# Other SBUF offsets for the operands of the matmuls: bytes left free in five pools

## The chip, the core and the metric

The kernel runs on one core of a Trainium2 chip. A core has a matrix engine (TensorE, PE in the profile; its weight loads are listed apart as PEld), a vector engine (VectorE, DVE), a scalar engine (ScalarE, ACT), a general engine (GpSimd, POOL) and a queue that issues most transfers (SyncE, SP). They share a memory of 128 partitions, SBUF; TensorE writes its results to a second memory, PSUM. The metric is the time of one execution on the device in microseconds (us), lower is better.

A matmul has two operands in SBUF. The *stationary* one (128 x 128 here) is loaded into the array by a weight load, the *moving* one (512, 384, 256 or 128 columns here) is then streamed past it. An address in this document is the byte offset of an operand within a partition, and an *offset* is that address modulo 256.

## The reference

One layer of a diffusion backbone, in float32, for 256 context tokens and 2048 latent tokens of width 1024:

```
h = rms_norm(x, norm1_g) * (1 + scale1) + shift1
q, k, v, f = split(h @ w_in)                      # 512 columns each
q, k = rms_norm(q), rms_norm(k)                   # rotary on the latent tokens
s = einsum('bqhmd,bkhmd->bhmqk', q, k) * scale    # 4 heads x 2 halves, 512 cached keys + 2048
p = softmax(s);  a = p[:, :, 0] - lam * p[:, :, 1]
attn = rms_norm(a @ v);  four = real(fft2(f)) @ w_four
x = x + gate1 * (concat(attn, four) @ w_out)
h = rms_norm(x, norm2_g) * (1 + scale2) + shift2
x = x + gate2 * (square(relu(h @ w1)) @ w2)       # 4096 hidden columns
```

The context tokens attend to themselves only. The modulation vectors come from `silu(c) @ w_mod + b_mod`. Outputs are the two groups of tokens and the new keys and values of the context.

## The kernel before

Each float32 product is made of three passes in the type fp32r: an operand is split into a high part and the rest, and `mm3` (lines 87 to 90) adds high x high (L88), high x low (L89) and low x high (L90) in PSUM. The stages follow each other and PE works through them in one order:

- **Projection** (33 to 476 us of the span): for each of 18 tiles of 128 tokens, four groups of 512 columns (`proj`). The activations `hh`, `hl` are stationary, the weights `wh`, `wl` are moving; products go to `pj`. 1728 matmuls of 512 columns on L88 to L90.
- **Fourier** part, to about 530 us; float32 matmuls without the split.
- **Attention** (530 to 1256 us): `fill` (L1065) multiplies a query tile `Q` (stationary) by 512 columns of keys `KS` (moving), 1272 matmuls into `Ss`. DVE takes the maxima (L1070), ACT the exponentials (L1089), POOL combines the two softmax halves (L1104, L1105), PE transposes the result (L1120, against the constant `ident`), ACT and DVE split it into `ah`, `al` (L1127, L1132), and PE multiplies by the values: `V` stationary, `ah` and `al` moving with 256 columns, 1536 matmuls on L88 to L90 into `po`. Keys, values and queries of a head are loaded by SP.
- **Output projection** (1256 to 1480 us): `mh`, `ml` stationary, the weights `woh`, `wol` moving with 512 columns, 864 matmuls, also into `po`. The weights' two halves of 512 output columns lie in different pools.
- **First MLP matrix** (1480 to 2184 us): seven products p = 1 to 7 of a Strassen scheme over blocks; the weights `oph..W`, `opl..W` are stationary, the tokens `mhh`, `mhl` are moving with 384 columns (L1728 to L1730), 4032 matmuls. p = 1 and 2 go to `pA`, 6 and 7 to `pB`, 5 and 3 to `pC`, 4 to `pD`. The tokens of p = 1 and 6 lie in the pool `hpa`, the others in the pools `hp[p]`.
- **Second MLP matrix** (2184 us to the end): the squared activations `sh`, `sl` are stationary and go round three buffers (`s_prep`: two in the pool `ms2s`, one in `t6`); the weights are moving with 512 columns and go round buffers in `ms2` (`oph..T`, `opl..T`) and in `y_w` (`th..T`, `tl..T`). 3024 matmuls on L88 to L90 into `ps`.

SBUF is handed out by pools. Pools of one side of the memory stand behind each other in the order in which they are opened, and the tiles of a pool in the order of their first use, so a byte more in one pool moves every tile behind it. Tiles start at multiples of 32 bytes. `reuse_waits="tile"` makes a new tile wait only for the users of the old tiles that it overlaps.

The lines that hand out the operands, among others:

```
qg, kg = cst("qg", [P, P]), cst("kg", [P, P])
t = ak.tile([P, self.nk], F32R, tag=f"KS{m}_{self.s}", name=f"KS{m}{self.nm}")
self.Q = at.tile([P, 2, 2, 256], F32R, tag="Q", name=f"Q{self.nm}", bufs=3)
mh = tm.tile([P, KD, P], F32R, tag="mh", name=f"mh{i}")
pool, bufs = (ms2s, 2) if m % 3 < 2 else (own["t6"], 1)
```

Of the kernel before, what the change touches and what calls it, by code (L numbers as in the profile page):

```python
# [11 lines left out]
F32 = mybir.dt.float32  # L12
# [7 lines left out]
P = 128  # L20
# [21 lines left out]
def body(tc, a, out):  # L42
    nc = tc.nc
    ctx = ExitStack()
    with ctx:
        const = ctx.enter_context(tc.tile_pool(name="const", bufs=1))
        dram = ctx.enter_context(tc.tile_pool(name="dram", bufs=1, space=DRAM))

        def cst(name, shape, dt=F32):
            return const.tile(shape, dt, tag=name, name=name)  # L50
# [27 lines left out]
        scale1 = cst("scale1", [P, KD, 2])  # L78
        scale2 = cst("scale2", [P, KD, 2])
        cols = cst("cols", [P, P])  # L80
        qg, kg = cst("qg", [P, P]), cst("kg", [P, P])
        nlam = cst("nlam", [P, 1])

        def pow_mhalf(dst, src, n):
            nc.gpsimd.tensor_tensor(dst, src, mhalf[:, :n], op=ALU.pow)
# [17 lines left out]
        def setup_cond(pool, pps, rows):  # L103
# [7 lines left out]
            nc.vector.tensor_copy(cols, pr)  # L111
            nc.vector.tensor_scalar_mul(cols[:, 96:97], cols[:, 96:97], 1.0 - LAM_INIT)

        def load_gains(pool):
            for t, n in ((qg, "q_norm_g"), (kg, "k_norm_g")):
                nc.gpsimd.dma_start(t[:, 0:64], a[n].partition_broadcast(P).rearrange("p o d -> p (o d)"))
            lq = pool.tile([P, 512], F32, tag="ff", name="lq", bufs=4)[:, 0:256].rearrange("p (n d) -> p n d", d=64)
            for i, n in enumerate(("lambda_q1", "lambda_q2", "lambda_k1", "lambda_k2")):
                nc.gpsimd.dma_start(lq[:, i, :], a[n].partition_broadcast(P).rearrange("p o d -> p (o d)"))
            return lq  # L120

        def setup_gains(pool, lq):
            for t, s in ((qg, 0.125), (kg, 1.0)):
                if s != 1.0:
                    nc.vector.tensor_scalar_mul(t[:, 0:64], t[:, 0:64], s)
                nc.vector.tensor_copy(
                    t[:, 64:128].rearrange("p (x h j) -> p x h j", h=2, j=16),
                    t[:, 0:64].rearrange("p (x h j) -> p x h j", h=2, j=16)[:, :, ::-1, :])
            nc.vector.tensor_mul(lq[:, 0:2, :], lq[:, 0:2, :], lq[:, 2:4, :])
            ls = pool.tile([P, 2], F32, tag="ls", name="ls")  # L130
            nc.vector.tensor_reduce(ls, lq[:, 0:2, :], axis=AX.X, op=ALU.add)
            nc.scalar.activation(ls, ls, AF.Exp)
            nc.vector.tensor_sub(nlam, ls[:, 1:2], ls[:, 0:1])
            nc.vector.tensor_scalar_add(nlam, nlam, -LAM_INIT)
# [111 lines left out]
        with ExitStack() as c1:  # L246
# [62 lines left out]
            def qk_post(i, ms=(0, 1), dst=None):  # L309
                s = i < 2  # L310
                if i not in RP:
                    rope_load(i)
                rp = RP.get(i)
                res = QK.setdefault(i, [])
                for m in ms:
                    gt = (qg, kg)[m]
                    if (i, m) not in QN:
                        qk_norm(i, m)
                    qn = QN.pop((i, m))
                    o = dst[m] if dst else po.tile([P, 512], F32, tag="qo", name=f"qo{i}_{m}", bufs=2)  # L320
                    if s:
                        nc.vector.tensor_mul(o.rearrange("p (g d) -> p g d", d=64),
                                             qn.rearrange("p (g d) -> p g d", d=64),
                                             gt[:, 0:64].unsqueeze(1).to_broadcast([P, 8, 64]))
                        if m == 1:
                            nc.sync.dma_start(out[2][i * P:i * P + P], o)
                    else:
                        tb = p1.tile([P, P], F32, tag="tb", name=f"tb{i}_{m}")
                        nc.vector.tensor_mul(tb, rp, gt)
                        nc.vector.tensor_mul(o.rearrange("p (g d) -> p g d", d=64),  # L330
                                             qn.rearrange("p (g d) -> p g d", d=64),
                                             tb[:, 0:64].unsqueeze(1).to_broadcast([P, 8, 64]))
                        t = t2(f"qt{i}_{m}")
                        tv = t.rearrange("p (g x h j) -> p x g h j", x=2, h=2, j=16)
                        qv = qn.rearrange("p (g x h j) -> p x g h j", x=2, h=2, j=16)
                        bv = tb[:, 64:128].rearrange("p (x h j) -> p x h j", h=2, j=16)
                        for x in range(2):
                            nc.vector.tensor_mul(tv[:, x], qv[:, x, :, ::-1, :],
                                                 bv[:, x].unsqueeze(1).to_broadcast([P, 8, 2, 16]))
                        nc.vector.tensor_add(o, o, t)  # L340
                    res.append(o)
# [111 lines left out]
            with tc.manual_schedule():  # L453
# [36 lines left out]
                with tc.tile_pool(name="p0h", bufs=6, reuse_waits="tile") as halves:  # L490
# [61 lines left out]
                    for k in range(KD):  # L552
# [20 lines left out]
                        if k in (1, 3):  # L573
                            b = k // 2
# [403 lines left out]
        with ExitStack() as c3_:  # L978
# [18 lines left out]
            class Head:  # L997
# [16 lines left out]
                def load_v(self):  # L1014
                    s, h, ak = self.s, self.h, self.ak
                    self.V = ak.tile([P, self.nkt, 2, P], F32R, tag=f"V_{s}", name=f"V{self.nm}")
                    nc.sync.dma_start(f32(self.V), vd[s][h])
                    self.vf = {}
                    if not s:
                        for kb in FULL:  # L1020
                            t = ak.tile([P, 2, P], F32, tag=f"vf{kb}", name=f"vf{kb}{self.nm}")
                            r = (kb - 4) * P
                            nc.sync.dma_start(t, vs[r:r + 2 * P, self.hc].rearrange("(t p) e -> p t e", p=P))
                            self.vf[kb] = t

            class Group:
                def __init__(self, hd, g):
# [423 lines left out]
        def h_parts(b, p):  # L1451

            src = HR.pop((b, p))
            pool = hpa if p in (1, 6) else hp[p]
            hi = pool.tile([P, 4, 384], F32R, tag=f"mhh{p}", name=f"mhh{b}_{p}")
            lo = pool.tile([P, 4, 384], F32R, tag=f"mhl{p}", name=f"mhl{b}_{p}")
            HO[b, p] = hi, lo
            src = src if isinstance(src, list) else [(slice(0, 4), src)]

            def high():  # L1460
# [45 lines left out]
        with c3o, ExitStack() as c4, ExitStack() as c4x, ExitStack() as c4w:  # L1506
# [2 lines left out]
            tm = c4.enter_context(tc.tile_pool(name="o_m", bufs=2, reuse_waits="tile"))  # L1509
            wl1 = c4.enter_context(tc.tile_pool(name="o_wl", bufs=1, reuse_waits="tile"))  # L1510
            t4 = c4.enter_context(tc.tile_pool(name="o_t", bufs=2, reuse_waits="tile"))
            wh1 = c4.enter_context(tc.tile_pool(name="o_wh", bufs=1, reuse_waits="tile"))
            tg = c4.enter_context(tc.tile_pool(name="o_g", bufs=2, reuse_waits="tile"))
            tx = c4x.enter_context(tc.tile_pool(name="o_x", bufs=2, reuse_waits="tile"))
# [172 lines left out]

        with c5r, ExitStack() as c5:
            hp.update((p, c5.enter_context(tc.tile_pool(name=f"m_h{p}", bufs=1, reuse_waits="tile"))) for p in (3, 4, 5, 7, 2))
            t5 = c5.enter_context(tc.tile_pool(name="m_t", bufs=2, reuse_waits="tile"))  # L1690
            pp = c5.enter_context(tc.tile_pool(name="m_p", bufs=2, space=PSUM, reuse_waits="tile"))
            PSB, U, G = {}, {}, {}
# [420 lines left out]
```

## Time and profile before

| | |
|---|---|
| median of 3 runs | 2883.29 us (2882.81 to 2885.51) |
| profiled execution | 2884.46 us |
| its span on the core | 2882.3 us |
| PE busy, with 15109 matmuls | 2849.2 us, 99% |
| weight loads (PEld) | 2465.0 us, 86% |
| DVE busy | 2017.5 us, 70% |
| ACT busy | 1547.8 us, 54% |
| POOL busy | 1063.5 us, 37% |
| granted TensorE clock | 0.999 of full speed |

A matmul's row in the trace lasts from its start to a modelled end, and the next one starts before that end. What a matmul costs PE in a dense stretch is therefore not the length of its row but the distance from its start to the start of the next one; below it is called the *interval*. PE counts as busy in the gap of up to some 160 ns that the modelled ends leave open. For the same reason a group's mean length (the second to last number of a row of groups) stands some 160 ns above the interval.

### The profile page before, as it was taken

The numbers are of one execution on the slowest core, as the hardware profiler recorded it, in microseconds if no ns is written. First come the engines' busy times: TensorE is split into PE (matmuls) and PEld (weight loads), VectorE is DVE, ScalarE is ACT, GpSimd is POOL, SyncE is SP. The second block draws the span as 40 slices with busy tenths as digits, with TensorE's granted clock in tenths as the row PEclk, the third lists the DMA queues.
The fourth block names the chain that finished last, engine by engine and source line by source line (L and its number), as shares of the span: only waits on it lengthen the run. The fifth ranks groups of instructions, "written<-read, shape, count | busy, mean of one in ns | idle before, by whom it ended". The sixth has DMA issues, their size and how long they took to land.

```text
span 2882.3 us, 43198 instructions
## 1 busy us (share of the span) xinstructions
PE 2849.2 (99%) x15109; PEld 2465.0 (86%) x15109; DVE 2017.5 (70%) x3376; ACT 1547.8 (54%) x3505; POOL 1063.5 (37%) x873
## 2 busy tenths in 40 slices
PE   8999999999999999999999999999999999999999
PEld 5888787688888888888889999999998888888887
DVE  7767776898988989864477777778775353445554
ACT  4333323798998989853356565556554332232221
POOL 1112113699998999942223333333331000000000
PEclk9999999999999999999999999999999999999999
DMA  7877887531211312036777677667747464345653
GB/s 283 216 194 190 228 210 229 191 112 38 72 69 46 113 38 98 21 116 204 241 215 236 218 247 229 219 220 240 227 166 254 146 201 139 132 143 186 206 199 110
DMA packets 392779, 492.93 MB, mean 171 GB/s; under 512 B 26467, under 2 KB 306384, under 8 KB 389490
## 3 DMA queue, kind: packets, MB, share of 16 engines
q1 hardware_dynamic: 387136, 479.73, 52.7%
q0 software_dynamic: 1872, 7.28, 0.8%
q10 hardware_dynamic: 3554, 3.17, 0.4%
q8 instruction: 119, 1.95, 0.3%
q14 instruction: 98, 0.80, 0.1%
HBM read 312.58 MB, written 179.59 MB: 171 GB/s over the span
## 4 chain that ended last, share of the span: by engine, by line
PE 91%; DVE 3%; DMA 2%; ACT 2%; issue 1%; POOL 0%; SPq 0%; ACTq 0%; DVEq 0%; POOLq 0%
PE Ss L1065 10%; PE ps L88 8%; PE ps L89 8%; PE ps L90 8%; PE pts L1120 5%; PE pj L88 4%; PE pj L89 4%; PE pj L90 4%; PE po L90 4%; PE po L88 4%; PE po L89 4%; PE pA L1728 2%; PE pA L1729 2%; PE pB L1729 2%; PE pB L1728 2%; PE pB L1730 2%
## 5 line engine op out<-in xcount | busy, mean ns | idle before, releaser
L1070 DVE TENSOR_REDUCE mxs<-Ss 128x1 f32<-128x512 f32 x636 | 413.2, 685 | 62.5 <-PE Ss L1065 50.6
L1405 DVE TENSOR_TENSOR sl<-sr,sh 128x768 fp32r<-128x768 f32 x168 | 161.7, 964 | 337.8 <-ACT sh L1404 336.3
L1105 POOL TENSOR_TENSOR P0s<-P0s,P1s 128x1024 f32<-128x1024 f32 (+2 forms) x128 | 378.7, 2958 | 10.7
L1404 ACT CAST sh<-sr 128x768 fp32r<-128x768 f32 x168 | 140.2, 836 | 424.8 <-PE ps L89 424.8
L1770 POOL TENSOR_TENSOR gs<-g,g 128x384 f32<-128x384 f32 x48 | 69.6, 1450 | 469.5 <-ACT g L1740 420.3
L88 PE MATMUL pj<-wh,hh 128*128 128x512 f32 x576 | 231.4, 402 | 4.5 <-DVE qn L305 2.4
L1089 ACT ACTIVATE P1s<-Ss,mxs 128x512 f32<-128x512 f32 x318 | 215.2, 694 | 36.1 <-DVE mxs L1073 36.1
L89 PE MATMUL ps<-tlT,sh 128*128 128x512 f32 x585 | 229.3, 392 | 0.0
L89 PE MATMUL pj<-wl,hh 128*128 128x512 f32 x576 | 229.2, 398 | 0.0
L88 PE MATMUL ps<-thT,sh 128*128 128x512 f32 x585 | 229.0, 391 | 0.0
L90 PE MATMUL pj<-wh,hl 128*128 128x512 f32 x576 | 228.8, 398 | 0.0
L90 PE MATMUL ps<-thT,sl 128*128 128x512 f32 x585 | 227.7, 389 | 0.0
L1089 ACT ACTIVATE P0s<-Ss,mxs 128x512 f32<-128x512 f32 x318 | 214.1, 690 | 5.5 <-DVE mxs L1073 4.8
L1065 PE MATMUL Ss<-KS1s,Qs 128*128 128x512 f32 x636 | 196.2, 420 | 5.8 <-ACT P0s L1089 3.1
L1065 PE MATMUL Ss<-KS0s,Qs 128*128 128x512 f32 x636 | 195.4, 420 | 2.4 <-ACT P1s L1089 2.4
L1120 PEld LDWEIGHTS pts<-ident,P0s 128*128 128x128 f32 x1280 | 157.7, 140 | 42.7 <-issue 2.1
L1120 PE MATMUL pts<-ident,P0s 128*128 128x128 f32 x1280 | 190.5, 272 | 0.7 <-ACT P1s L1089 0.7
L1739 ACT ACTIVATE g<-uz 128x384 f32<-128x384 f32 x144 | 75.8, 527 | 200.9 <-DVE uz L1762 174.4
L1104 POOL TENSOR_SCALAR P1s<-P1s,tots 128x1024 f32<-128x1024 f32 (+2 forms) x128 | 171.8, 1342 | 5.8
L1132 DVE TENSOR_TENSOR als<-pts,ahs 128x512 fp32r<-128x512 f32 x256 | 165.9, 681 | 6.9 <-ACT ahs L1127 6.6
L88 PE MATMUL ps<-ophT,sh 128*128 128x512 f32 x423 | 165.7, 392 | 1.1 <-DVE uz L1762 1.1
L90 PE MATMUL ps<-ophT,sl 128*128 128x512 f32 x423 | 165.7, 392 | 0.0
(536 smaller groups left out, 8057.5 us busy)
## 6 DMA issues: line engine op xcount, KB each, us to landing
sr<-sd SPq DMA_DIRECT2D x84, 768.0 KB
a<-in_w SPq DMA_DIRECT2D x184, 256.0 KB
sd<-gs SPq DMA_DIRECT2D x192, 192.0 KB
sd<-g SPq DMA_DIRECT2D x144, 192.0 KB
wm<-in_w_mod SPq DMA_DIRECT2D x32, 512.0 KB
Qs<-qd SPq DMA_DIRECT2D x32, 512.0 KB
b<-in_w SPq DMA_DIRECT2D x64, 256.0 KB
b<-tsum SPq DMA_DIRECT2D x64, 256.0 KB
```

Of the source, the lines that this page charges most:

```text
L88: nc.tensor.matmul(ps, lh, rh, start=first, stop=False)
L89: nc.tensor.matmul(ps, lh, rl, start=False, stop=False)
L90: nc.tensor.matmul(ps, ll, rh, start=False, stop=last)
L1065: nc.tensor.matmul(S[:, :w], self.Q[:, x, m, j * P:j * P + P], self.hd.KS[m][:, b * 512:b * 512 + w], start=(x == 0), stop=(x == 1))
L1070: nc.vector.tensor_reduce(self.mx[j][:, m, b:b + 1], self.S[j, m, b], axis=AX.X, op=ALU.max)
L1089: nc.scalar.activation(dst, S, AF.Exp, bias=self.mx[j][:, m, 6:7], accum_out=self.sm[j][:, m, b:b + 1])
L1104: nc.gpsimd.tensor_scalar(p, p, tot[:, 3:4], 0.0, op0=ALU.mult, op1=ALU.add)
L1105: nc.gpsimd.tensor_add(d, d, p)
L1120: nc.tensor.transpose(pt[:, c:c + P], self.p0[j][:, (kb + t) * P:(kb + t + 1) * P], ident)
L1132: nc.vector.tensor_sub(t, self.pt[kb], f32(self.A[kb][0]))
L1404: nc.scalar.copy(hi, src)
L1405: nc.vector.tensor_sub(lo, src, f32(hi))
```

## The change

The change adds a helper `shift` that takes a tile nobody uses out of a pool, calls it in seven places, and takes the two gain tiles `qg`, `kg` out of the pool of constants and into `p1`. No instruction is added, removed or moved: the instructions of PE, DVE, ACT, POOL and SP stand in the same order in both programs, and the waits of PE and DVE are the same too. Because a few tiles now overlap other old tiles, one semaphore wait less stands before two ACT exponentials and one POOL addition of the first attention groups and before a load of context keys on SP, and one wait for POOL more before one ACT cast (`mhh` of p = 7, first block, L1462).

```
@@ -78,8 +78,13 @@
-        qg, kg = cst("qg", [P, P]), cst("kg", [P, P])
         nlam = cst("nlam", [P, 1])
+
+        def shift(pool, nbytes, nm):
+
+            pool.tile([P, nbytes // 4], F32, tag=f"shift{nm}", name=f"shift{nm}", bufs=1)
+
+        shift(const, 192, "c")
@@ -111,7 +116,12 @@
+        GN = []
+
         def load_gains(pool):
+            shift(pool, 64, "p")
+            GN.extend(pool.tile([P, P], F32, tag=f"{x}g", name=f"{x}g", bufs=1) for x in "qk")
+            qg, kg = GN
@@ -120,7 +130,7 @@
-            for t, s in ((qg, 0.125), (kg, 1.0)):
+            for t, s in zip(GN, (0.125, 1.0)):
@@ -313,7 +323,7 @@
-                    gt = (qg, kg)[m]
+                    gt = GN[m]
@@ -1022,6 +1032,8 @@
                             self.vf[kb] = t
+                        if h == 0:
+                            shift(ak, 192, "k")
@@ -1452,9 +1464,13 @@
             pool = hpa if p in (1, 6) else hp[p]
+            if pool is hpa and not b and p == 6:
+                shift(hpa, 64, "a")
             hi = pool.tile([P, 4, 384], F32R, tag=f"mhh{p}", name=f"mhh{b}_{p}")
             lo = pool.tile([P, 4, 384], F32R, tag=f"mhl{p}", name=f"mhl{b}_{p}")
             HO[b, p] = hi, lo
+            if pool is hpa and not b and p == 6:
+                shift(hpa, 64, "b")
@@ -1509,6 +1525,7 @@
             t4 = c4.enter_context(tc.tile_pool(name="o_t", bufs=2, reuse_waits="tile"))
+            shift(t4, 128, "o")
@@ -1687,6 +1704,7 @@
             hp.update((p, c5.enter_context(tc.tile_pool(name=f"m_h{p}", bufs=1, reuse_waits="tile"))) for p in (3, 4, 5, 7, 2))
+            shift(hp[3], 64, "h")
```

What comes of it are other offsets. This table is worked out from the addresses that the pools gave in the two built programs; "distance" is the stationary operand's offset less the moving one's, modulo 256.

| matmuls, columns | moving | stationary | before: moving / stationary, distance | after |
|---|---|---|---|---|
| projection, 1728 x 512 | wh, wl | hh, hl | 224 / 32, 64 | 224 / 224, 0 |
| scores, 1272 x 512 | KS | Q | 160 / 32, 128 | 224 / 224, 0 |
| attention by values, 1536 x 256 | ah, al | V | 96 / 160, 64 | 32 / 224, 192 |
| transposes of P0, 1280 x 128 | ident | P0 | 128 / 32, 160 | 128 / 224, 96 |
| output projection, columns 512 to 1023, 288 x 512 | woh | mh, ml | 160 / 32, 128 | 224 / 224, 0 |
| the same, 144 x 512 | wol | mh | 32 / 32, 0 | 224 / 224, 0 |
| output projection, columns 0 to 511, 432 x 512 | woh, wol | mh, ml | 160 / 32, 128 | 224 / 224, 0 |
| first MLP matrix, p = 1 (`pA`), 576 x 384 | mhh, mhl | ophW, oplW | 224 / 224, 0 | 96 / 224, 128 |
| first MLP matrix, p = 6 (`pB`), 576 x 384 | mhh, mhl | ophW, oplW | 224 / 224, 0 | 160 / 224, 64 |
| first MLP matrix, the rest, 2880 x 384 | mhh, mhl | ophW, oplW | 32 / 224, 192 | 32 / 224, 192 |
| second MLP matrix, 846 x 512 | ophT, oplT | sh, sl in `ms2s` | 224 / 224, 0 | 224 / 224, 0 |
| second MLP matrix, 423 x 512 | ophT, oplT | sh, sl in `t6` | 224 / 32, 64 | 224 / 224, 0 |
| second MLP matrix, 1170 x 512 | thT, tlT | sh, sl in `ms2s` | 32 / 224, 192 | 224 / 224, 0 |
| second MLP matrix, 585 x 512 | thT, tlT | sh, sl in `t6` | 32 / 32, 0 | 224 / 224, 0 |

Every tile that moves does so by a multiple of 64 bytes; addresses in PSUM do not change.

## The prediction

> **What bounds the kernel now.** I read the page's busy shares and its chain first, then the stages.
>
> ```profile
> PE 2849.2 (99%) x15109; PEld 2465.0 (86%) x15109; DVE 2017.5 (70%) x3376; ACT 1547.8 (54%) x3505; POOL 1063.5 (37%) x873
> ...
> PE 91%; DVE 3%; DMA 2%; ACT 2%; issue 1%; POOL 0%; SPq 0%; ACTq 0%; DVEq 0%; POOLq 0%
> ```
>
> PE is busy for 99% of the span and is 91% of the chain that ended last. A change without a single new instruction can gain only where PE's own instructions follow each other faster. The stages, from the windows view (projection; attention; output projection; first and second MLP matrix):
>
> ```profile
> core 0: us, PE busy (x) PEld busy (x) DVE busy (x) ACT busy (x) POOL busy (x), PEclk, DMA share, GB/s
> 33.00:480.00 447.00, 444.22 (x2053) 360.03 (x2054) 322.93 (x586) 154.19 (x329) 86.39 (x68) 0.99 0.78 208
> 565.00:1256.00 691.00, 685.40 (x4470) 590.95 (x4469) 611.90 (x1196) 618.28 (x1729) 627.37 (x506) 1.00 0.19 65
> 1256.00:1480.00 224.00, 222.34 (x1071) 183.24 (x1070) 121.12 (x163) 90.68 (x211) 59.60 (x54) 1.00 0.70 215
> 1480.00:2184.00 704.00, 702.42 (x4044) 700.81 (x4043) 537.51 (x823) 419.55 (x786) 239.22 (x189) 1.00 0.68 223
> 2184.00:2882.00 698.00, 692.82 (x3026) 567.65 (x3024) 329.89 (x434) 204.04 (x290) 5.75 (x4) 1.00 0.51 168
> ```
>
> Four of the five leave the other engines at 76% or less and the transfers at 0.78, so time that PE saves there is saved. In attention DVE, ACT and POOL are at 89 to 91%: a gain there may partly turn into waiting. The clock stands at 0.99 to 1.00 everywhere, so it explains no difference between stages.
>
> **Does the offset matter?** The second MLP matrix answers it, since its three buffers of `sh` alternate between two offsets within a few microseconds, with the same instructions. From the timeline, the first matmul of each stretch:
>
> ```profile
> 2296.82 0.39 PE L88 MATMUL ps<-ophT,sh 128*128 128x512 f32 x1
> 2304.99 0.40 PE L88 MATMUL ps<-ophT,sh 128*128 128x512 f32 x1
> 2309.19 0.39 PE L88 MATMUL ps<-ophT,sh 128*128 128x512 f32 x1
> 2315.34 0.40 PE L88 MATMUL ps<-thT,sh 128*128 128x512 f32 x1
> 2317.42 0.39 PE L88 MATMUL ps<-thT,sh 128*128 128x512 f32 x1
> 2321.51 0.39 PE L88 MATMUL ps<-thT,sh 128*128 128x512 f32 x1
> 2329.75 0.39 PE L88 MATMUL ps<-ophT,sh 128*128 128x512 f32 x1
> ```
>
> One buffer serves 18 matmuls (two k, three row tiles, three passes). By the table of offsets, the first stretch is 36 matmuls at distance 0: 8.17 us / 36 = 226.9 ns each. Then 18 at distance 64: 4.20 / 18 = 233.3. Then 27 at distance 0: 6.15 / 27 = 227.8. After nine more at 192 come 18 at distance 0 with other weights: 4.09 / 18 = 227.2, and 36 at 192: 8.24 / 36 = 228.9. So distance 0 costs 227.4, distance 64 costs 5.9 ns more, distance 192 costs 1.5 more. Distance 128 shows in the output projection, where one half of the weights has `wol` at distance 0 and the other half has not:
>
> ```profile
> 1290.15 0.39 PE L89 MATMUL po<-wol,mh 128*128 128x512 f32 x1
> 1294.96 0.39 PE L89 MATMUL po<-wol,mh 128*128 128x512 f32 x1
> 1295.18 0.39 PE L90 MATMUL po<-woh,ml 128*128 128x512 f32 x1
> 1300.06 0.40 PE L90 MATMUL po<-woh,ml 128*128 128x512 f32 x1
> ```
>
> Seven triples with one matmul at distance 0: 4.81 / 21 = 229.0 ns on average. Seven triples at distance 128 throughout: 4.88 / 21 = 232.4. The neighbours of a matmul share in its gain, so I use averages over triples alone. These differences repeat each time a buffer comes round, under the same clock and instructions: I take the distance as their cause.
>
> **The change, part by part.** Intervals after the change are taken as 227.4 for all 512-column matmuls.
>
> *Projection.* All 1728 stand at distance 64. A dense run of 54 of them, up to the next transpose:
>
> ```profile
> 150.18 0.39 PE L90 MATMUL pj<-wh,hl 128*128 128x512 f32 x1
> 162.78 0.38 PE L347 MATMUL ptckT<-ident,ck 128*128 128x128 f32 x2
> ```
>
> 12.60 / 54 = 233.3, exactly the price of distance 64 above, though DVE and the transfers are far busier here. 1728 x 5.9 = **10.2 us**. DVE (72%) and ACT (34%) keep up.
>
> *Second MLP matrix.* 423 x 5.9 = 2.5 and 1170 x 1.5 = 1.8, together **4.3 us**. 1431 matmuls stay at distance 0.
>
> *Output projection.* 432 x (229.0 - 227.4) + 432 x (232.4 - 227.4) = 0.7 + 2.2 = **2.9 us**.
>
> *Scores.* 1272 at distance 128. In the view by source line, minimum / median / maximum length:
>
> ```profile
> L89 PE MATMUL ps<-oplT,sh x423: 387/389/398, 2184.4 to 2877.3; 128*128 128x512 f32 x141
> L89 PE MATMUL pj<-wl,hh x576: 388/394/628, 33.8 to 475.8; 128*128 128x512 f32 x192
> L1065 PE MATMUL Ss<-KS0s,Qs x636: 387/397/505, 530.1 to 1222.6; 128*128 128x512 f32 x159
> ```
>
> A row's length follows its interval: the median is 389 where most are at distance 0, 394 at distance 64, 397 in the scores. So they do pay; I take the 5.0 ns of distance 128: 1272 x 5.0 = 6.4 us of PE work. How much is kept is open, since PE waits here:
>
> ```profile
> 853.53 0.63 PE L1065 MATMUL Ss<-KS0s,Qs 128*128 128x512 f32 x2
> 853.99 0.27 PE L1120 MATMUL pts<-ident,P0s 128*128 128x128 f32 x1
> ...
> 854.78 0.28 PE L88 MATMUL po<-ahs,Vs 128*128 128x256 f32 x1
> 855.69 0.28 PE L90 MATMUL po<-ahs,Vs 128*128 128x256 f32 x1
> 856.07 0.73 PE L1065 MATMUL Ss<-KS1s,Qs 128*128 128x512 f32 x2
> ```
>
> Two scores take 0.46 us, eight value matmuls 0.91 (114 ns each), but the ninth is followed only after 0.38 us: some 0.26 us in which PE waits for ACT and DVE to free a score buffer, hidden under the modelled ends and counted as busy. Such waits shrink with nothing that PE saves if they come from ACT and DVE. With those at 90% I keep two thirds: **4.2 us** (bounds 0 and 6.4).
>
> *Values.* 1536 matmuls of 256 columns go from distance 64 to 192. No row shows 192 at this size. By the 512-column rows it would gain 4.4 ns; but the 114 above is already near what streaming 256 columns takes (227.4 / 2 = 113.7), which leaves little. Bounds: a gain of 2 ns (from a mean near 116) or a loss of as much as 6, the size of the step at 512 columns; within a stage that waits. I take **0**, bounds -3 and +9 us.
>
> *First MLP matrix.* 1152 matmuls of 384 columns leave distance 0, half for 128, half for 64. First matmuls of twelve:
>
> ```profile
> 1484.89 0.33 PE L1728 MATMUL pA<-mhh,ophW 128*128 128x384 f32 x1
> 1486.96 0.34 PE L1728 MATMUL pB<-mhh,ophW 128*128 128x384 f32 x1
> ...
> 1495.24 0.34 PE L1728 MATMUL pA<-mhh,ophW 128*128 128x384 f32 x1
> 1497.35 0.33 PE L1728 MATMUL pB<-mhh,ophW 128*128 128x384 f32 x1
> 1499.43 0.33 PE L1728 MATMUL pC<-mhh,ophW 128*128 128x384 f32 x1
> ```
>
> Distance 192 costs 2.07 / 12 = 172.5; distance 0 costs 2.11 / 12 = 175.8 in `pA` but 2.08 / 12 = 173.3 in `pB`. So here distance 0 is no advantage, and more than the offset plays a part. Best case: `pA` falls to 173, 576 x 2.5 = 1.4 us gained. Worst case: both pay what 64 and 128 cost at 512 columns over a floor of 173, 576 x (5.9 + 5.0 - 2.5) = 4.8 us lost. The stage has no cover, PE is all of it. I take a loss of **2.0 us**, a little over the middle of the two, the nearest rows at those distances being the 512-column ones.
>
> *Transposes.* They change their distance too, but their length is the same where the operand stands at 32 (`P0s`) and at 224 (`qo`), so nothing is put in:
>
> ```profile
> L1120 PE MATMUL pts<-ident,P0s 128*128 128x128 f32 x1280 | 190.5, 272 | 0.7 <-ACT P1s L1089 0.7
> L347 PE MATMUL ptqT<-ident,qo 128*128 128x128 f32 x64 | 9.6, 272 | 0.0
> ```
>
> *Waits.* The dropped ones concern transfers long landed; the new wait of one ACT cast is for POOL work of the stage before. Nothing.
>
> *Sum.* -10.2 - 4.3 - 2.9 - 4.2 + 0 + 2.0 = -19.6 us. The profiled execution took 2884.5 (span 2882.3 and 2.2 around it), 1.2 above the median of 2883.3; 2884.5 - 19.6 - 1.2 = 2863.7, so **2864 us**. Extremes of this case: all gains kept and the best bounds, -10.2 - 4.3 - 2.9 - 6.4 - 3 - 1.4 = -28.2 (2855); scores worth nothing, the values two thirds of their loss and the first MLP its worst, -17.4 + 6 + 4.8 = -6.6 (2877).
>
> [...]
>
> **The rivals.**
>
> *Only alternation shows a cause.* Projection and scores never alternate; their 233 and 232 could come from the denser traffic of DVE, ACT and transfers. Then only -4.3 - 2.9 + 2.0 = -5.2 remains: 2878. Against it: 233.3 is met to the tenth in a stage with half the DVE load. 0.09.
>
> *No effect.* The third buffer could be slow for where it lies, not for its offset (an area of memory beyond the 256 bytes, as the two figures of `pA` and `pB` at equal distance suggest). Then the new addresses draw anew: about 2883. Against it: `sh`, `wol` and the projection lie in quite different places and agree. 0.05. [...]
>
> *Slower: another engine in attention.* Every tile of that stage moves, those of POOL too:
>
> ```profile
> L1105 POOL TENSOR_TENSOR P0s<-P0s,P1s 128x1024 f32<-128x1024 f32 (+2 forms) x128 | 378.7, 2958 | 10.7
> ```
>
> POOL is busy for 627 of 691 us. Were its instructions to lengthen by 10% they would fill the stage, and from about 14% on they outweigh the gain: at 15%, 721 - 691 = 30 us more, less 15.4 kept elsewhere: 2898. Against it: both of its tiles move by the same 832 bytes. 0.04.
>
> **Chances.** The likeliest case 0.82 (about 0.02 of it less than 0.2% faster). 0.2% (5.8 us) is about what a measurement of this kernel can tell from no change. Faster 0.80 + 0.04 of the first rival = 0.84; same 0.02 + 0.05 + 0.04 = 0.11; slower 0.05, with 0.01 of the second. The range takes the likeliest case's bounds, cut at 2876 above: 2855 to 2876.
>
> **What would show it.** The lengths of `pj` and `Ss` rows fall to a median of 389; the stretches of `ps` lose their steps; the projection ends some 10 us earlier; `pA`/`pB` rows of 336 move up if 384 columns pay. I am wrong if `pj` keeps 394, if attention's 691 us don't shrink, or if the first MLP stage grows beyond 709.

## The result, and the profile after

The changed kernel takes 2871.26 us (median of 6 runs, 2869.99 to 2873.0) against 2883.53 us before (6 runs, 2882.81 to 2885.51). The ratio is 0.9957, with a 95% interval of 0.9944 to 0.9970: 12.3 us less. 2864 us were predicted, with a range of 2855 to 2876.

The profiled execution of the changed kernel took 2872.75 us, with a span of 2870.6. The changed file is longer at the top: `mm3` is now on lines 93 to 95, the scores are on L1077, the first MLP matrix on L1746 to L1748. The busy shares and the chain of the page of after:

```profile
PE 2836.0 (99%) x15109; PEld 2471.3 (86%) x15109; DVE 2015.4 (70%) x3376; ACT 1548.1 (54%) x3505; POOL 1063.7 (37%) x873
...
PE 54%; DVE 1%; DMA 0%; issue 0%; ACT 0%; SPq 0%; POOL 0%; DVEq 0%; POOLq 0%
```

PE lost 13.2 us of busy time, DVE 2.1, ACT and POOL did not change by more than 0.3, and the weight loads gained 6.3; the number of instructions is the same. The shares of the chain add up to 55% here, so it was followed only about half way back; what it holds is PE.

Where the time went is read best from the first matmul of each stage (projection, end of the projection, output projection, first and second MLP matrix). The timeline of before:

```profile
33.20 0.80 PE L88 MATMUL pj<-wh,hh 128*128 128x512 f32 x1 [1.98 <-DVE hh L544]
476.24 1.02 PE L777 MATMUL pabE<-c,E 128*128 128x256 f32 x4
1256.21 0.39 PE L88 MATMUL po<-woh,mh 128*128 128x512 f32 x1
1480.70 0.34 PE L1728 MATMUL pA<-mhh,ophW 128*128 128x384 f32 x1
2184.14 0.39 PE L88 MATMUL ps<-ophT,sh 128*128 128x512 f32 x1
```

and the timeline of after:

```profile
33.15 0.79 PE L93 MATMUL pj<-wh,hh 128*128 128x512 f32 x1 [1.98 <-DVE hh L554]
470.29 1.89 PE L787 MATMUL pabE<-c,E 128*128 128x256 f32 x8
1251.54 0.39 PE L93 MATMUL po<-woh,mh 128*128 128x512 f32 x1
1473.69 0.34 PE L1746 MATMUL pA<-mhh,ophW 128*128 128x384 f32 x1
2179.19 0.39 PE L93 MATMUL ps<-ophT,sh 128*128 128x512 f32 x1
```

The differences of these starts, and of the end of the last matmul, against the terms that were predicted:

| stage | predicted, us | measured, us |
|---|---|---|
| projection | -10.2 | -5.9 |
| Fourier part and attention (scores -4.2, values 0) | -4.2 | +1.3 |
| output projection | -2.9 | -2.3 |
| first MLP matrix | +2.0 | +2.05 |
| second MLP matrix | -4.3 | -6.8 |
| sum | -19.6 | -11.7 |

So the projection gave little more than half of its term, the scores gave nothing, and the term of the second MLP matrix was too small. The windows view of after, the same five stages as before the change:

```profile
core 0: us, PE busy (x) PEld busy (x) DVE busy (x) ACT busy (x) POOL busy (x), PEclk, DMA share, GB/s
33.00:472.00 439.00, 434.28 (x2042) 359.81 (x2043) 320.94 (x583) 153.94 (x329) 84.92 (x66) 0.99 0.78 209
559.00:1251.00 692.00, 686.99 (x4468) 593.68 (x4467) 611.82 (x1195) 618.04 (x1728) 627.64 (x506) 1.00 0.19 65
1251.00:1474.00 223.00, 221.24 (x1078) 184.12 (x1078) 121.57 (x165) 91.96 (x212) 59.60 (x54) 1.00 0.70 217
1474.00:2179.00 705.00, 703.48 (x4039) 702.04 (x4038) 535.25 (x823) 418.77 (x785) 239.28 (x189) 1.00 0.68 222
2179.00:2870.00 691.00, 686.09 (x3027) 567.49 (x3025) 329.83 (x434) 204.39 (x290) 5.75 (x4) 1.00 0.51 170
```

Attention is the stage that stands out: DVE, ACT and POOL do what they did (611.82, 618.04 and 627.64 us against 611.90, 618.28 and 627.37), and PE is busy longer than before (686.99 us of a window of 692 against 685.40 of 691). The view by source line (minimum / median / maximum length in ns) says which matmuls got shorter. The prediction shows the rows of `pj` and `Ss` before; the first row here is the one of `ps` before, the other three are after:

```profile
L89 PE MATMUL ps<-tlT,sh x585: 387/394/397, 2204.3 to 2875.9; 128*128 128x512 f32 x195
L94 PE MATMUL ps<-tlT,sh x585: 389/389/389, 2199.2 to 2864.2; 128*128 128x512 f32 x195
L94 PE MATMUL pj<-wl,hh x576: 387/389/632, 33.7 to 469.8; 128*128 128x512 f32 x192
L1077 PE MATMUL Ss<-KS0s,Qs x636: 387/397/506, 524.1 to 1217.9; 128*128 128x512 f32 x159
```

This group of `ps` is now 389 in every single row, where it went from 387 to 397: the steps between its buffers are gone. `pj` fell from a median of 394 to 389. The scores stand at distance 0 as well, and their median is still 397. The prediction had read this 397 as the price of distance 128.

Worked out over all dense matmuls, the intervals went from 233.3 to 227.5 ns in `pj`, and from 227.4, 229.2 and 233.3 (distances 0, 192 and 64) to 226.7 in `ps`, but stayed between 232 and 233 in the scores. The values (256 columns, 64 to 192) went from 116.1 to 117.5.

### The profile page after: what moved, and what is told of

Read it like the earlier page. It is cut to its first block, busy times and chain, and to the rows that moved or that the text cites. A ratio compares the mean times of both kernels' runs of the same rounds, so it can differ in the third digit from the quotient of the medians.

```text
span 2870.6 us, 43195 instructions
## 1 busy us (share of the span) xinstructions
PE 2836.0 (99%) x15109; PEld 2471.3 (86%) x15109; DVE 2015.4 (70%) x3376; ACT 1548.1 (54%) x3505; POOL 1063.7 (37%) x873
## 4 chain that ended last, share of the span: by engine, by line
PE 54%; DVE 1%; DMA 0%; issue 0%; ACT 0%; SPq 0%; POOL 0%; DVEq 0%; POOLq 0%
PE ps L93 8%; PE ps L94 8%; PE ps L95 8%; PE pB L1747 2%; PE pB L1746 2%; PE pB L1748 2%; PE pA L1746 2%; PE pA L1748 2%; PE pA L1747 2%; PE pC L1747 2%; PE pC L1746 2%; PE pC L1748 2%; PE po L93 2%; PE po L95 2%; PE po L94 2%; PE pD L1748 1%
## 5 line engine op out<-in xcount | busy, mean ns | idle before, releaser
L94 PE MATMUL pj<-wl,hh 128*128 128x512 f32 x576 | 227.4, 395 | 0.3 <-DVE wl L515 0.3
L95 PE MATMUL pj<-wh,hl 128*128 128x512 f32 x576 | 226.9, 395 | 0.0
L1077 PE MATMUL Ss<-KS1s,Qs 128*128 128x512 f32 x636 | 196.6, 421 | 5.4 <-ACT P0s L1101 3.2
L1077 PE MATMUL Ss<-KS0s,Qs 128*128 128x512 f32 x636 | 195.4, 420 | 2.4 <-ACT P1s L1101 2.4
L94 PE MATMUL ps<-oplT,sh 128*128 128x512 f32 x423 | 164.6, 389 | 0.0
```

What stands on the lines that cost most here:

```text
L94: nc.tensor.matmul(ps, lh, rl, start=False, stop=False)
L95: nc.tensor.matmul(ps, ll, rh, start=False, stop=last)
L1077: nc.tensor.matmul(S[:, :w], self.Q[:, x, m, j * P:j * P + P], self.hd.KS[m][:, b * 512:b * 512 + w], start=(x == 0), stop=(x == 1))
```

## The experiments

Two things were open: why the scores gained nothing (theory A: a stream of matmuls needs some length before it runs at its distance's price), and where some 4 us of the projection went. Stage times below are found as above, from one profiled execution each.

### Streams by themselves

A program that leaves out the whole layer and writes zeros: runs of matmuls with operands at chosen distances, four transposes between two runs, and next to nothing on the other engines.

```
def run(ps, n, d, r, at):
    for k in range(r):
        x, m = (at + k) % 24, (at + k) % 6 * 512
        nc.tensor.matmul(ps[:, 0:n], sta[:, x * P + d // 4:x * P + d // 4 + P], mov[:, m:m + n],
                         start=(k == 0), stop=(k == r - 1))
LONG = [(n, d, 48) for n in (512, 384, 256) for d in range(0, 256, 32)]
SHORT = [(512, d, r) for r in (2, 4, 8, 12) for d in (0, 64, 128, 192)]
```

> A kernel that leaves the whole layer out (its outputs are zeros) and only streams fp32r matmuls past stationary operands whose offset stands at a chosen distance from the moving one's: 48 matmuls in a row for 512, 384 and 256 columns at eight distances from 0 to 224, then 512 columns at distances 0, 64, 128, 192 in runs of 2, 4, 8 and 12, always with four float32 transposes between runs. Theory A (a stream settles): a stream at distance 0 starts at 230 to 235 ns per matmul and settles to 226.7 after about eight, one at distance 64 stays at 233.3. Then runs of 48 at 512 columns show 227.5 at distance 0, 233.3 at 64, 232 at 128, 229 at 192, and runs of 2 and 4 show 231 to 235 at every distance. Rival B (the distance acts on each matmul alone, and the scores are slow for what else goes on in attention): runs of 2 and 4 at distance 0 show 227, at 64 show 233. At 384 columns both expect 173.3 at distances 0 and 192, about 177 at 64 and 175 at 128; at 256 columns 116 at 64 and 117.5 at 192.

The timeline of this program puts a run together into one row. These are the runs of 48 at distances 0, 64 and 128, each with the transposes behind it, and the first run of two at distance 0:

```profile
122.84 11.18 PE L89 MATMUL bank<-mov,sta 128*128 128x512 f32 x48
133.86 0.60 PE L83 MATMUL tr<-ident,raw 128*128 128x128 f32 x4
...
145.84 11.45 PE L89 MATMUL bank<-mov,sta 128*128 128x512 f32 x48
157.13 0.60 PE L83 MATMUL tr<-ident,raw 128*128 128x128 f32 x4
...
169.17 11.40 PE L89 MATMUL bank<-mov,sta 128*128 128x512 f32 x48
180.41 0.60 PE L83 MATMUL tr<-ident,raw 128*128 128x128 f32 x4
...
335.00 0.72 PE L89 MATMUL bank<-mov,sta 128*128 128x512 f32 x2
335.55 0.60 PE L83 MATMUL tr<-ident,raw 128*128 128x128 f32 x4
```

From a run's start to the start of the transposes: 11.02 us / 48 = 229.6 ns at distance 0, 11.29 / 48 = 235.2 at 64, 11.24 / 48 = 234.2 at 128. So the distance matters with the other engines and the transfers all but idle (from 100 to 600 us DVE is busy for 2.77 us, ACT and POOL for 0, at a DMA share of 0.00). Within the run of distance 0 the intervals go 314, 235, 234, 236, 224, 231, 235, 229, 232, 231 and only then stay at 226.7; some runs of twelve are there after six intervals. The intervals of the second half of each run of 48, in ns:

| distance | 0 | 32 | 64 | 96 | 128 | 160 | 192 | 224 |
|---|---|---|---|---|---|---|---|---|
| 512 columns | 226.7 | 233.3 | 233.3 | 234.2 | 232.1 | 233.3 | 228.9 | 233.3 |
| 384 columns | 173.3 | 173.3 | 173.3 | 173.3 | 176.1 | 176.7 | 173.3 | 176.7 |
| 256 columns | 120.0 | 118.3 | 117.8 | 117.4 | 118.7 | 120.0 | 117.8 | 116.7 |

And the mean time from a run's start to the transposes, for short runs of 512 columns, in ns:

| run of | distance 0 | 64 | 128 | 192 |
|---|---|---|---|---|
| 2 | 545.9 | 552.5 | 547.5 | 548.1 |
| 4 | 1015.5 | 1019.3 | 1011.7 | 1018.3 |
| 8 | 1938 | 1952 | 1945 | 1932 |
| 12 | 2850 | 2883 | 2878 | 2851 |

In runs of two, distance 0 is 0.8 ns per matmul better than distance 128, in runs of four 0.95 worse: nothing. In runs of twelve it is 2.3 ns per matmul better, in runs of 48 4.6. Some 250 of the 1272 scores stand in runs of two and some 950 in runs of four between other matmuls, so this is why they gained nothing. The kernel agrees where it has one long run, at the start of attention. Its first intervals after the change are 314, 229, 234, 236, 224, 231, 235, 229, 232, 231 and then 226 or 227 up to the first wait; before the change, at distance 128, they are 229 and 237 in turn up to that wait. That short runs are cheap at distance 0 on a quiet chip, and only attention's other engines take the gain away, is ruled out by the streams. What makes a stream settle is not shown.

The table also supports the prediction's prices for long streams (233.3, 228.9 and 232.1 against 226.7), and it shows that 384 and 256 columns have an order of their own. Three figures did not come as expected: 384 columns at distance 64 cost 173.3 and not 177, and 256 columns cost 117.8 at distance 64 as at 192. So these plain streams do not show the 1.4 ns by which the kernel's values, which come in triples, got longer.

### The first MLP matrix at distance 192

The tokens of p = 1 and 6 go to the distance that the other five products have. The rest is as in the change.

```
             if pool is hpa and not b and p == 6:
-                shift(hpa, 64, "a")
...
-                shift(hpa, 64, "b")
+                shift(hpa, 192, "b")
```

> The change, but the tokens of products 1 and 6 of the first MLP matrix start at offset 32 instead of 96 and 160, so that all 4032 matmuls of 384 columns stand at distance 192. If the distance sets their price, the 576 of pA fall from 175.3 to 173.3 ns and the 576 of pB from 177.2 to 173.3: the stage shrinks by 1.2 + 2.2 = 3.4 us, to about 702 us from its first to the second matrix's first matmul, and the kernel takes about 2868 us. If higher address bits set it, pA keeps about 175 and the stage shrinks by 2 us or less. The projection's clock drop, if it is the rule for the changed offsets, shows here again at some 302 us; if it is a matter of chance, it need not.

2868.96 us (4 runs, 2867.35 to 2872.03), ratio to before 0.995 (0.9933 to 0.9967). The stage is 0.98 us shorter than before the change and 3.0 shorter than after it, and all its dense matmuls stand at 173.3 ns. So the loss of the first MLP matrix comes from the two new distances. The first matmuls of twelve in the timeline of after show which one it is:

```profile
1488.17 0.33 PE L1746 MATMUL pA<-mhh,ophW 128*128 128x384 f32 x1
1490.28 0.34 PE L1746 MATMUL pB<-mhh,ophW 128*128 128x384 f32 x1
1492.40 0.34 PE L1746 MATMUL pC<-mhh,ophW 128*128 128x384 f32 x1
```

`pA` at distance 128 takes 2.11 us for twelve, as it did at distance 0. `pB` at distance 64 takes 2.12, where it took 2.08: over all of p = 6 the interval went from 173.3 to about 177.2, 576 x 3.9 = 2.2 us. The whole loss is `pB`'s. `pA` paid some 2 ns above 173.3 at distance 0 already and pays the same at 128; at 192 it loses them, which is why this version is shorter than before. Why distance 0 cost `pA` more than `pB` is not shown.

### A lighter DVE in the projection

Two kernels, before and after the change, each with seven of the eight `macc` steps of a modulation column left out. This takes work from DVE in the projection, and leaves the modulation of the second half of the layer incomplete.

```
-                for k in range(KD):
+                for k in range(1):
```

> The kernel before, with seven of eight steps of the modulation sums on DVE left out in the projection (the modulation vectors of the second half of the layer are then not the reference's); the order of work is that of the next kernel. Its projection stage, first to last projected tile, is to be compared with the next one's alone. Expected shorter than the 443.0 us of the kernel before, since DVE is late less often.

> The changed kernel with the same steps left out. Theory A: the projection gained 5.9 us instead of 10.2 since PE, when faster, waited longer at four places for DVE (at 56, 201, 299 and 351 us), and one of these waits let the clock drop. Without the late DVE work the stage is 9 to 10 us shorter than in the kernel with the old offsets beside it. Rival: the offsets are worth less in the projection than the intervals say; then the difference stays near 6 us.

2898.3 us without the change and 2895.19 with it, one run each. Both are slower than the full kernels: the scheduler put the rest of the work in another order, and the projection came out 8.5 and 8.1 us longer than that of the kernel before, with stretches at half the clock in both (mean granted clock 0.997 and 0.996). Nor was the wait for DVE shorter: for `qn` alone it is 8.8 and 11.0 us, against 3.7 in the kernel before. So the pair does not show what a lighter DVE would return; for that the experiment would have had to keep the order of the work. Against each other the two have the same order on PE, and they differ by 0.4 us in the projection, not by the 9 to 10 expected nor by the rival's 6. The dense intervals gave -9.1 us again; 6.65 came back in waits and transposes and 2.1 at half the clock.

### The change in the projection alone

The constants and `p1` as in the change, the five other shifts left out, and a pool of 832 bytes opened behind the projection, so that the tiles of the later stages lie where they did before.

```
+        pad = ctx.enter_context(tc.tile_pool(name="pad", bufs=1, reuse_waits="tile"))
+        shift(pad, 832, "x")
...
-                        if h == 0:
-                            shift(ak, 192, "k")
...
-            shift(t4, 128, "o")
...
-            shift(hp[3], 64, "h")
```

> The change in the projection alone: its tiles lie as in the changed kernel, and 832 bytes left free behind it put every tile of the later stages where it was before. If the parts add up, the projection (first to last projected tile) is 5.9 to 7.8 us shorter than the 443.0 us before, as in the two kernels with the new offsets so far, and the times from there on are those of before within 0.3 us: scores and values 691.1, output projection 224.5, first MLP matrix 703.4, the second 693.8; the kernel takes 2875.5 to 2877.5 us. Rival (tiles of different stages act on each other, for instance through transfers that start earlier): a later stage moves by over 1 us.

2877.05 us (8 runs), ratio 0.9975 (0.9965 to 0.9985). The projection is 7.7 us shorter, and every later stage is within 0.07 us of its time before. So the parts do not act on each other across stages, and what the projection loses of its 10 us it loses within itself.

### Attention undone

The first MLP matrix at 192, as above, and the tiles of attention back at their old offsets.

```
+            shift(at, 64, "q")
...
-                        if h == 0:
-                            shift(ak, 192, "k")
```

> The change with the first MLP matrix at distance 192 throughout, and with the tiles of attention at their old offsets (keys 160, queries 32, values 160, ah and al 96). Theory A: scores stand in runs of two and four between transposes, never settle, and gained nothing from distance 0, while the 256-column matmuls lost 1.5 ns each by distance 192 (116.0 to 117.5). Then attention takes 691.1 us again, 1.3 to 1.6 less than with the new offsets, the scores' interval is 232.3 instead of 233.0, and the kernel takes about 2867 us, the fastest so far. Rival: attention's extra 1.3 us came from elsewhere (the smaller distance to the projection, transfers); then it stays at 692.5.

2866.38 us (5 runs, 2866.05 to 2869.34), ratio 0.9939 (0.9927 to 0.9952). Attention takes its old time again to 0.04 us, the values 115.5 ns, the scores between 232 and 233 as in all versions. So attention's 1.3 us were lost to its new offsets. This is the fastest of the versions, 0.6% below the kernel before, and its interval overlaps that of the change.

### Only the values undone

The kernel with the first MLP matrix at 192, with only the values moved back to distance 64; the scores stay at distance 0.

```
+                    if not s and h < 2:
+                        shift(ak, 128, "v")
...
-                        if h == 0:
-                            shift(ak, 192, "k")
+                        if h < 2:
+                            shift(ak, (64, 128)[h], "k")
```

> Against the second run of this study (first MLP's second pool at distance 192) only the values' operand V moves: the values' 256-column matmuls go back from distance 192 to 64, the scores stay at distance 0. The attention stage there was 1.55 us longer than in the kernel before, with both undone 0.03 us shorter. Theory A (settling): scores in runs of two to four get nothing from distance 0, and what attention lost is mostly the values: their mean interval in the windows of eight falls from 117.5 back to about 116.0 ns, attention ends up 0.2 to 0.7 us longer than before, and the time is 2867 to 2868.5. Rival: the loss is the scores' (233.0 against 232.3 ns at distance 0 in runs of two, 1272 x 0.7 = 0.9 us): then values at distance 64 change nothing, attention stays 1.2 to 1.6 us longer than before, time about 2869.

2867.56 us (4 runs, 2867.03 to 2869.48), ratio 0.9941 (0.9924 to 0.9957). The values fall to 115.4 ns, and from the first value matmul to the end of attention the stage is 0.75 us longer than before, where it was 1.55 with both moved (1.3 in the two profiles of the change). So the values make about half of the loss. The transposes, whose distance also changed, do not keep the rest: from that matmul on, the intervals that begin with a transpose sum to 117.5 us before and here, those of the scores to 306.5 before (306.7 and 306.9 in two more profiles with the old offsets) and 307.55 here. The streams program has a loss of this size: with 0.95 ns more for each of some 950 scores in runs of four and 0.8 less for each of some 250 in runs of two, distance 0 costs an estimated 0.7 us. In this one profile another 2.2 us were lost ahead of the first value matmul, 1.6 of them when the clock fell (below).

### The change once more

The changed kernel again, for a second profile of its projection.

> The changed kernel once more, for its profile. If the drop of the clock in the projection comes with the changed offsets, it shows again at some 302 us and the projection takes 437.1 us; if the wait of 2.4 us there only sometimes meets a window of the clock's control, it need not, and then the projection takes about 435.3 us as in the kernel with the first MLP matrix at 192. All other stages are the same to 0.2 us.

2869.83 us (one run). All later stages agree with the first profile of after to 0.05 us; the projection is 8.8 us shorter than before instead of 5.9, at 434.3 us shorter than either case expected. So the projection differs between these two executions by more than any other stage.

### Triples, and the address above the 256 bytes

As the first program, but in the order of `mm3` (high x high, high x low, low x high), and with 0, 1024, 4096 or 8192 bytes more in the address of the high stationary operands. The layer is left out again.

```
nc.tensor.matmul(ps[:, 0:n], sh, mh, start=(x == 0), stop=False)
nc.tensor.matmul(ps[:, 0:n], sh, ml, start=False, stop=False)
nc.tensor.matmul(ps[:, 0:n], sl, mh, start=False, stop=(x == groups - 1))
```

> Again the layer is left out (outputs are not written by it, but zeros). Streams of 48 matmuls in the order of the split products (high x high, high x low, low x high), at 512 and 384 columns, distances 0, 64, 128, 192, and with 0, 1024, 4096 and 8192 bytes more between the high stationary operands and the moving ones, which leaves the distance modulo 256 as it is. If the distance alone sets the pace once a stream has settled, the four rows of one distance agree to 0.5 ns: at 512 columns 226.7, 233.3, 232, 229. If more address bits matter, rows of one distance differ; at 384 columns I expect that, since distance 64 settled at 173.3 in the first streams and took 177 in the kernel.

Settled intervals in ns, lowest and highest of the four addresses:

| distance | 0 | 64 | 128 | 192 |
|---|---|---|---|---|
| 512 columns | 226.7 | 233.3 | 232.1 to 233.3 | 228.9 |
| 384 columns | 173.3 | 174.5 to 176.7 | 175.5 to 176.1 | 173.3 |

So at distances 0 and 192 the address above the 256 bytes made no difference, and at 64 and 128 it made 2.1 ns at most. The rival by which a buffer is slow for where it lies, and not for its distance, falls at 512 columns. At 384 columns the distance is not all: distance 64 costs 1.2 to 3.3 ns in triples and nothing in the plain runs. The two programs differ in the order of the operands and in their addresses, and which of the two does it was not told apart. The kernel's `pB`, in triples, pays 3.9.

### Where the projection's time went

This compares the six profiles with the new projection offsets and the full work, instruction by instruction, with the profile of before. Each of the 2034 instructions of PE in the stage is put into one of three groups: dense ones; those that ran while the granted clock was at half in either profile; and the transposes and the matmuls that are followed by a wait.

| profile | dense | half clock | waits, transposes | stage, us |
|---|---|---|---|---|
| the change | -9.4 | +1.6 | +1.9 | -5.9 |
| attention undone | -9.4 | +1.55 | +1.8 | -6.05 |
| first MLP matrix at 192 | -9.5 | -0.35 | +2.1 | -7.7 |
| projection alone | -9.5 | -0.7 | +2.5 | -7.7 |
| values undone | -9.45 | +0.1 | +1.5 | -7.85 |
| the change once more | -9.5 | -1.0 | +1.7 | -8.8 |

The dense intervals gave 9.4 to 9.5 us in all six, close to the 10.2 predicted. 1.5 to 2.5 us of it came back as waits. The waits of the weight loads in the projection, before (us in total, times, longest):

```profile
PEld pj L88 <- DVE qn L305: 3.7, 3, 2.1
PEld pj L88 <- DVE hh L544: 2.1, 1, 2.1
PEld pj L89 <- DVE wl L505: 0.5, 1, 0.5
```

and after:

```profile
PEld pj L93 <- DVE qn L315: 5.3, 3, 2.4
PEld pj L93 <- DVE hh L554: 2.1, 1, 2.1
PEld pj L94 <- DVE wl L515: 0.8, 1, 0.8
```

The wait for `qn` grew by 1.6 us: in its three places, at 203, 301 and 353 us of after, by 0.3, 0.3 and 1.05. At each of them `qn` starts right behind the same POOL step. The chain of the longest stands in the timeline of after at 297 to 302 us:

```profile
297.37 0.16 DVE L301 TENSOR_SCALAR qss<-qss 128x16 f32<-128x16 f32 x1
...
297.68 2.91 POOL L302 TENSOR_TENSOR qrs<-qss,mhalf 128x16 f32<-128x16 f32 x1 [4.25 <-DVE qss L301]
...
300.62 0.69 DVE L315 TENSOR_TENSOR qn<-pj,qrs 128x512 f32<-128x512 f32 x1 [1.88 <-POOL qrs L302]
...
301.36 0.54 PE L93 MATMUL pj<-wh,hh 128*128 128x512 f32 x1 [2.01 <-DVE qn L315]
```

DVE sums the squares, POOL takes 2.91 us for the root of 16 numbers, DVE scales with it and so empties `pj`, and only then can PE write there. None of these steps is faster than before by more than 0.01 us (there, from 302 us on, they took 0.17, 2.91 and 0.69), so a PE that comes earlier waits longer, here 2.43 us of the weight loads against 2.15. DVE's mean share of 72% does not show this: at this place DVE itself waits 1.88 us for POOL. That a shorter POOL step would return the rest of the gain was not tried.

The third part is the clock. Behind that wait it is at half for 3.41 us in the windows view of after (columns as in the windows view above; the clock is the third number from the end):

```profile
298.28:301.69 3.41, 1.40 (x6) 0.86 (x5) 1.50 (x3) 1.16 (x2) 2.30 (x1) 1.00 1.00 197
301.69:305.10 3.41, 3.41 (x9) 2.66 (x8) 3.41 (x8) 0.00 (x0) 0.00 (x0) 0.50 0.90 205
```

Eight matmuls took 427 ns in place of about 230, 1.6 us. It happened in two of the six profiles, and the wait of the change once more, 2.4 us of the weight loads like this one, was followed by full clock:

```profile
296.03:299.44 3.41, 2.94 (x13) 2.08 (x12) 2.28 (x5) 1.21 (x2) 2.19 (x1) 1.00 0.98 193
299.44:302.85 3.41, 1.92 (x8) 1.61 (x9) 2.63 (x6) 0.00 (x0) 0.71 (x1) 1.00 1.01 165
302.85:306.27 3.42, 3.42 (x16) 2.82 (x15) 3.42 (x9) 0.00 (x0) 0.00 (x0) 1.00 0.90 299
```

These windows are cut at the clock's own steps. In each profile the granted clock changes only at times that lie a whole number of 3.413 us apart: the slow stretches of after begin at 32.04 and 301.69 us, 79 such steps apart, and those of values undone at 32.22 and 554.46, 153 steps. Cut at these steps, the wait of after falls into one window whole, and PE idles for 2.01 of its 3.41 us; in the second profile a step cuts the wait into 0.47 and 1.50. Over the nine profiles of the layer, from 40 us to the last matmul, each of the ten windows at full clock in which PE idled for 2.00 us or more (by the profile's modelled ends) is followed by one at half, and none of those with 1.89 or less. So in these profiles the 1.6 us went with where the wait fell on the steps, and that differed between the two executions of the same kernel. The stage also begins with some matmuls at half clock, before the change too (12 there, 7 to 12 in the others); their number makes the negative and the small entries of that column.

## Why the prediction was right or wrong

- **Does the offset matter?** Right. The prices read from adjacent stretches of `ps` (0, +1.5, +5.9 ns) return a little larger in the program of streams alone (226.7, 228.9, 233.3: 0, +2.2, +6.6).
- **Projection, -10.2, measured -5.9 to -8.8.** The price per matmul was right (dense part -9.4 to -9.5). The step that failed is the sentence that DVE and ACT keep up: it was argued from mean busy shares, while the view of waits already showed PE waiting for `qn`. 1.5 to 2.5 us went there, and up to 1.6 to the clock.
- **Second MLP matrix, -4.3, measured -6.8.** The mechanism was right, the term too small. The price after the change was taken as 227.4, the average of the distance-0 stretches before. Those came behind stretches at other distances; with all of them at distance 0, every matmul runs at 226.7. Distance 192 averaged 229.2 rather than 228.9. By these, (227.4 - 226.7) x 1431 + (233.3 - 226.7) x 423 + (229.2 - 226.7) x 1170 = 6.7.
- **Output projection, -2.9, measured -2.3.** Right in kind. Its intervals after, 226.9 to 228.3 on the three lines of `mm3`, lie on average a little above the 227.4 assumed.
- **Scores, -4.2, measured nothing or a small loss.** This is the step that cost the prediction most. The 5 ns were taken from the long streams of the output projection and applied to runs of two to four, where the streams program shows no gain. The median length of 397, read as proof that the scores pay for distance 128, is what an unsettled run shows at distance 0 as well. The caution about DVE and ACT pointed at the wrong reason.
- **Values, 0, a loss of about 0.8 us.** Inside the bounds given. Taking them back returned 0.8 us, though 1280 dense intervals became 2.1 ns shorter each, 2.7 us in all: PE's waits among the values took 1.3 us of that back.
- **First MLP matrix, +2.0, measured +2.05.** Right in size by luck: 2.0 was near the middle between a best and a worst case, and neither came. `pA` pays nothing for leaving distance 0 and gains nothing, `pB` loses all of it.
- **The rivals.** Only alternation shows a cause: fell, the projection's dense intervals did drop. No effect: fell at 512 columns; at 384 its hint, that `pA` and `pB` differ at equal distance, stays unexplained. Another engine in attention: fell, POOL's 627 us did not change.

The total came out above the forecast because 4.3 us of the projection, 5.5 of attention and 0.6 of the output projection were missing, and only 2.5 of the second MLP matrix came on top. It lies inside the range because the range allowed the scores to be worth nothing, though for another reason.

## What to carry to other kernels

A price per matmul read from long streams must not be put on runs of two to four (in the streams distance 0 beat 128 by 4.6 ns per matmul in runs of 48 and by 0.8 in runs of two, and lost 0.95 in runs of four): look first at how many follow each other without a break, and take the price from rows of that length. When PE gets faster in a stage, go through the waits that PE already has there, since the chain behind each of them does not get faster (the POOL step ahead of `qn` took 2.91 us before and after, and PE's weight loads waited 5.3 us for `qn` in place of 3.7), and a mean busy share, here DVE's 72%, does not show it. And compare operands at every width that the kernel uses, in the order in which it uses them: here distance 0 was the best at 512 columns (226.7 ns), but the kernel's `pA` at 384 ran faster at 192 (173.3, some 2 less than at 0), and in the plain streams of 256 columns 0 was among the dearest (120.0, against 116.7 at 224).

## What the runs showed of the hardware that was not expected

- In the streams of 512 columns of fp32r, a run at distance 0 behind transposes took 224 to 236 ns for up to nine intervals, after a first one of about 315, and 226.7 after them; at distance 64 the average stayed at 233.3.
- The distance with the lowest price differed with the width: in plain runs it was 0 at 512 columns (226.7), 0, 32, 64, 96 or 192 at 384 (173.3), 224 at 256 (116.7).
- In the nine profiles of the layer, from 40 us to the last matmul, the granted clock was at half in the window of 3.41 us behind each of the ten full-clock windows in which PE idled for 2.00 us or more, and behind none of those with 1.89 or less. The clearest case is a wait of 2.00 us of the scores for ACT, 31 us into attention, that stands in the profile of before too (ending at 561.42 us) and in all the others. With the values undone it falls into one window whole, and the next one is slow; before the change a step cuts it into 1.65 and 0.35, and the clock stays. The timeline and the windows view of the kernel with the values undone:

```profile
554.06 0.90 PE L1079 MATMUL Ss<-KS0s,Qs 128*128 128x512 f32 x2 [2.00 <-ACT P1s L1103]
```

```profile
551.05:554.46 3.41, 1.41 (x7) 0.79 (x7) 3.06 (x6) 2.39 (x7) 3.23 (x4) 1.00 0.39 125
554.46:557.88 3.42, 3.42 (x13) 2.73 (x12) 1.70 (x3) 2.71 (x9) 3.34 (x3) 0.50 0.11 36
```

Left open: what in the hardware makes the distance count, why a stream has to settle, why 384 and 256 columns order the distances in another way, what besides the distance counts at 384 columns, and what made the kernel's values dearer at 192 than at 64.
